# Merge and output projection as a planned list, their loads through the tile of x, the first two row blocks in two parts

## The chip, the core and the metric

The kernel runs on one core of a Trainium2 chip. The metric is the device time of one execution in microseconds (us). The core has five engines that work side by side: PE (TensorE, matmuls), DVE (VectorE), ACT (ScalarE), POOL (GpSimd) and SP (SyncE, which here issues nearly all DMA transfers). Each takes its instructions in a fixed order; semaphores tie them together.

## What is computed

One layer of a diffusion backbone over 512 tokens of width 1024: a token mixer (a long convolution of width 512 and an RWKV-7 recurrence of width 512, merged by gates, then an output projection) and an expert-choice mixture of 16 experts. What matters here is the end of the mixer and the start of the experts:

```python
y_hy = hyena_branch(hy_cols, p) @ p['hy_proj']                 # (512, 512) @ (512, 1024)
y_rw, finals = rwkv_branch(rw_cols, p, states0)
g_hy, g_rw = jnp.split(jax.nn.sigmoid(gate_cols), 2, axis=-1)
mixed = (g_hy * y_hy + g_rw * (y_rw @ p['rw_proj'])) @ p['w_out']   # (512, 1024) @ (1024, 1024)
x = x + m_lat[2] * rmsnorm(mixed, p['norm1_post'])
h2 = rmsnorm(x, p['norm2_pre']) * (1.0 + m_lat[4]) + m_lat[3]
x = x + m_lat[5] * rmsnorm(expert_choice_moe(h2, p), p['norm2_post'])
# expert_choice_moe: softmax(h2 @ router_w); each expert takes its 64 best tokens; SwiGLU of width 2048
```

## The kernel before

The kernel runs through sections one after the other. Norm, modulation and the Hyena branch come first; the branch leaves its result in DRAM as u_d. Then comes the RWKV section. Its instructions are not issued as they are written: while `plan.on` is set, an object `Plan` records them (`Plan.add`, with an estimated cost and latency for each), and `Plan.run` sorts them by a list scheduler (for each engine, the instruction that can start first, and among those the one with the longest chain behind it) and issues them in that order inside `tc.manual_schedule()`. Consecutive matmuls that nothing cuts apart are one operation of the list; `cut()` ends such an operation. Because the issue goes through that one place, all instructions of this section stand under line 313 in the profile. The section also computes the gate columns (`gates`, lines around 890): weights of w_in pass through two raw tiles of 512 KB, the tanh of the result goes by a staging tile `stg` to g_d in DRAM. The recurrence's result, after its epilogue, goes to y_d.

Behind it, from line 1296 on, stands what the change edits. These instructions are not planned by hand; the framework's own scheduler orders them, and it may issue them between those of the list.

- Merge (lines 1352 to 1382): q = 0 for the Hyena branch (u_d, hy_proj), q = 1 for RWKV (y_d, rw_proj). Each input of 128 x 512 and each weight block of 128 x 1024 is loaded into one of two raw tiles (pool `raw`, NRAW = 2) and split by `parts` into a high part (rounded to fp32r, on ACT) and a low part (the rest, on DVE). `mm3` multiplies high by high, high by low and low by high, 12 matmuls for each of 8 column blocks i. For q = 0 the gated result goes to `first` (the place of `xn`), for q = 1 the two are added on POOL and split again into `mixT`.
- The weights' parts stand in the five 2 MB places of pool `w2p`: hy_proj in 0 and 1, rw_proj in 2 and 3, the halves of w_out in 4, 0 and 1, 2. The expert weights use these five places after that, two of `w3p` and the one of x (`xp`), eight in all, in turn; the first in turn before is place 3.
- Output projection (lines 1385 to 1431): for each of four row blocks n of 128 tokens and each half q of 512 channels, 24 matmuls over 8 channel blocks k into one of four PSUM banks; then the norm (Square on ACT with its sum, Sqrt, reciprocal), scaling and adding to x on DVE, transposes, the router's matmuls `pl`, and the norm of the new x.
- Router and experts (from line 1440 on, unchanged): softmax, the 64 best tokens of each expert by eight rounds of MAX8 and MATCH_REPLACE8 on DVE, then for each of 8 pairs of experts a gather by one-hot matmuls (`px`), three weight loads of 2 MB for each quarter of an expert (lines 1513 and 1516) and the matmuls `ph` and `py`.

Pools of the framework are placed on the left or the right side of SBUF. A pool that takes over the place of a closed one waits for all of it, unless it is opened with `reuse_waits="tile"`, as the RWKV section's pool `rw` is; then each tile waits for the tiles that it overlaps alone.

## Time and profile before

| | |
|---|---|
| median of 3 runs | 1858.79 us (1856.28 to 1859.96) |
| profiled execution | 1859.19 us |
| its span, first to last instruction | 1857.4 us |
| mean granted TensorE clock | 0.944 |
| PE, DVE, ACT, POOL busy | 86%, 35%, 20%, 11% |
| RWKV section | about 350 to 741 us |
| merge and output projection | about 741 to 870 us |
| router and experts | about 870 to 1857 us |

Times in the rows are microseconds from the span's start unless marked ns. L328, L333, L334, L337, L340 and L370 are helper lines (matmul, ACT copy, ACT function, tensor by tensor, scalar-tensor-tensor, transpose); what an instruction is for is read from its tile names, out<-in. `ppr` is the merge's PSUM, `po` that of the output projection, `gg` the gate tile, `mixh` and `mixl` the parts of mixT, `yr` and `yh` an input and its high part, `exp_w` an expert's weights. PEclk is the granted clock as a share of 2.4 GHz. A bracket holds the idle time of the engine ahead of the instruction and what ended it.

### The profile page before, as it was taken

Reading aid. Unit: us, or ns where it says so; the run is one execution under the profiler, and the core shown is the slowest. Engines: PE = TensorE matmul, PEld = TensorE weight load, DVE = VectorE, ACT = ScalarE, POOL = GpSimd, SP = SyncE. Lnnn points to the kernel's source line nnn. Section 1 sums busy time; section 2 is a strip of 40 time slices with the busy share of each in tenths; the row PEclk is TensorE's granted clock in tenths of the full one; section 3 lists DMA queues with packets and bytes.
Section 4 is the critical chain, followed back from the end, with each engine's and each line's share of the span. In section 5 each row is a group of like instructions: output and inputs, shape, how many; then the busy total and the mean of one; then the engine's idle time right before and its main releaser. Section 6 shows DMA issues by size and latency. Waiting matters only on the chain.

```text
span 1857.4 us, 33304 instructions
## 1 busy us (share of the span) xinstructions
PE 1600.7 (86%) x14486; PEld 1054.1 (57%) x14486; DVE 643.1 (35%) x1230; ACT 373.2 (20%) x773; POOL 209.0 (11%) x222
## 2 busy tenths in 40 slices
PE   7898899777788999688699989989899898998985
PEld 3456676555666776477565545455454554555542
DVE  3765665566776533454402002011020110200203
ACT  4444432232343212233000000000000000000001
POOL 0534201312333201020000000000000000000001
PEclk8799899888898999799799999999999999999998
DMA  7455443465554532754699999999999999999995
GB/s 289 142 178 187 159 151 131 145 158 133 118 124 121 140 81 82 253 176 185 287 427 426 427 427 427 425 427 426 428 426 427 426 426 427 427 427 427 426 426 228
DMA packets 168382, 537.36 MB, mean 289 GB/s; under 512 B 96827, under 2 KB 110795, under 8 KB 143404
## 3 DMA queue, kind: packets, MB, share of 16 engines
q1 hardware_dynamic: 166064, 531.72, 74.5%
q10 hardware_dynamic: 2172, 3.51, 0.6%
q8 instruction: 114, 1.87, 0.4%
q14 instruction: 32, 0.26, 0.0%
HBM read 507.89 MB, written 27.30 MB: 288 GB/s over the span
## 4 chain that ended last, share of the span: by engine, by line
PE 40%; DMA 14%; DVE 3%; issue 1%; ACT 1%; POOL 0%; DVEq 0%; SPq 0%; ACTq 0%; POOLq 0%
PE ph L328 18%; DMA exp_w<-in_exp_w 12%; PE py L328 10%; PE px L328 3%; PE pso L328 3%; PE po L328 2%; PE pht L370 1%; DVE hd L337 1%; ACT hT L333 1%; PE ppr L328 1%; PE pl L328 0%; PE pbq L328 0%; PE pbp L328 0%; POOL gg L337 0%; DMA gg<-g_d 0%
## 5 line engine op out<-in xcount | busy, mean ns | idle before, releaser
L328 PE MATMUL ph<-exp_w,xe 128*64 128x256 f32 x4096 | 470.0, 381 | 25.3 <-DMA exp_w<-in_exp_w 25.3
L328 PEld LDWEIGHTS ph<-exp_w,xe 128*64 128x64 f32 x4096 | 319.0, 137 | 193.9 <-issue 66.5
L337 DVE TENSOR_TENSOR hd<-ph,hd 128x256 f32<-128x256 f32 x64 | 27.2, 425 | 672.8 <-PE ph L328 672.8
L328 PE MATMUL py<-exp_w,hT 128*64 128x512 f32 x1024 | 236.8, 598 | 24.6 <-ACT hT L333 24.6
L313 PE MATMUL psfl<-hh,raw 128*128 128x256 f32 x512 | 149.6, 423 | 14.9 <-DMA raw<-in_w_in 8.5
L328 PEld LDWEIGHTS py<-exp_w,hT 128*64 128x64 f32 x1024 | 78.3, 136 | 138.4 <-issue 92.8
L313 PEld LDWEIGHTS psfl<-hh,raw 128*128 128x128 f32 x512 | 95.9, 204 | 37.9 <-issue 16.1
L334 ACT ACTIVATE hd<-ph 128x256 f32<-128x256 f32 x64 | 24.6, 384 | 432.6 <-PE ph L328 432.6
L333 ACT ACTIVATE hT<-pht 128x256 f32<-128x256 f32 x64 | 24.6, 384 | 283.6 <-PE pht L370 283.6
L328 PEld LDWEIGHTS px<-OH,xn 128*128 128x128 f32 x512 | 66.2, 198 | 23.4 <-issue 22.4
L1495 POOL COPY sel<-kcon 16x128 f32<-16x128 f32 x8 | 2.2, 283 | 609.4 <-PE pbq L328 609.4
L328 PE MATMUL pso<-ye,oT 128*128 128x512 f32 x128 | 69.5, 634 | 0.7 <-ACT ye L333 0.7
L328 PE MATMUL px<-OH,xn 128*128 128x128 f32 x512 | 68.5, 283 | 0.9 <-DVE OH L344 0.9
L370 PE MATMUL pht<-kcon,hd 128*128 128x128 f32 x128 | 28.0, 300 | 36.1 <-DVE hd L337 35.9
L337 DVE TENSOR_TENSOR mo<-pso,mo 128x512 f32<-128x512 f32 x56 | 38.4, 691 | 40.9 <-PE pso L328 40.9
L370 PEld LDWEIGHTS pht<-kcon,hd 128*128 128x128 f32 x128 | 12.8, 140 | 65.1 <-DVE hd L337 65.1
L337 POOL TENSOR_TENSOR mw<-mw 128x256 f32<-128x256 f32 x32 | 35.0, 1110 | 97.0 <-DVE mw L340 90.8
L1539 DVE COPY ye<-py 64x512 f32<-64x512 f32 x16 | 11.1, 693 | 95.7 <-ACT ye L333 95.7
L313 DVE TENSOR_TENSOR M<-pssc,kcon 128x256 f32<-128x256 f32 x80 | 29.2, 416 | 24.8 <-PE pssc L313 23.5
L340 DVE SCALAR_TENSOR_TENSOR mw<-mw,sc,mw 128x256 f32<-128x256 f32 x64 | 28.5, 493 | 22.9 <-DMA mw<-in_mod_w 21.4
L328 PE MATMUL phy<-ha,wh_h 128*128 128x512 f32 x96 | 31.0, 455 | 1.9 <-ACT wh_h L333 1.8
L313 PE MATMUL pslv<-XX,M 32*32 32x32 f32 x1152 | 17.6, 209 | 16.0 <-issue 7.4
(383 smaller groups left out, 2227.3 us busy)
## 6 DMA issues: line engine op xcount, KB each, us to landing
exp_w<-in_exp_w SPq DMA_DIRECT2D x192, 2048.0 KB
mw<-in_mod_w SPq DMA_DIRECT2D x48, 512.0 KB
raw<-in_w_in SPq DMA_DIRECT2D x32, 512.0 KB
w_h<-in_w_in SPq DMA_DIRECT2D x12, 512.0 KB
w_c<-in_w_in SPq DMA_DIRECT2D x12, 512.0 KB
k<-k_d SPq DMA_DIRECT2D x8, 768.0 KB
g_d<-stg SPq DMA_DIRECT2D x16, 256.0 KB
gg<-g_d SPq DMA_DIRECT2D x16, 256.0 KB
```

The lines of the kernel that those rows point to most:

```text
L313: f(*a, **k)
L328: return TE.matmul(*a, **k)
L333: return A.activation(out, in_, func, scale=scale, **kw)
L334: return A.activation(out, in_, func, bias=bias, scale=scale, **kw)
L337: e.tensor_tensor(out, a, b, op=op)
L340: V.scalar_tensor_tensor(out, a, s, b, op0=op0, op1=op1)
L370: TE.transpose(out, in_, ident[0:n, 0:n])
L1495: G.tensor_copy(sel, ident[0:NE, 2 * q:2 * q + 2].rearrange("p (a b) -> p a b", b=1).to_broadcast([NE, 2, CAP]))
L1539: V.tensor_copy(ye[r, 512:1024], py[64:128, :])
```

## The change

Merge and output projection are recorded and issued by `Plan` as well, in a second list. Six places of 512 KB take their loads up to the twelfth (four of them in the tile of x, which is itself loaded later, and the two raw tiles), two after that; all loads go by SP. The first two row blocks are projected from channel blocks 0 to 5 first and from 6 and 7 later. The adds of the last three column blocks go to DVE. The ring of half-row tiles has five (NGT) and serves gates, scaled halves, transposed halves and the throw-away outputs of Square. Six pools now wait tile by tile, x's pool is on the right side, and four buffers of the RWKV section are created earlier. The planner's costs change too, for both lists: matmul operations, DMA cost (now the time that its bytes take) and latency (2.0 us), and no latency between two operations of PE. The diff, without the parts that only move a definition; from `first = xn` on the lines taken out (printed above) are left away:

```diff
-NGT = 3
+NGT = 5
...
-                place, t = None, 0.2 if what == "transpose" else size * (0.00055 if single else 0.00175) + 0.02
+                place, t = None, 0.2 if what == "transpose" else size * (0.00043 if single else 0.00175) + 0.015
             else:
                 place, t = (lhs.offset // lhs.ap[0][0], out.offset // out.ap[0][0]), 0.116 * size / 64
             if self.open is None:
-                self.open = dict(e=engine, calls=[], cost=0.15, small=[], lat=0.35, reads=[], writes=[])
+                self.open = dict(e=engine, calls=[], cost=0.05, small=[], lat=0.35, reads=[], writes=[])
                 self.ops.append(self.open)
...
-            cost, lat = 0.07, 2.2 + size / (180e3 if run >= 512 else 60e3)
+
+            cost, lat = max(0.07, size / (380e3 if run >= 512 else 100e3)), 2.0
...
-                o["cost"] += sum(t for _, t in o["small"]) / min(4, len(set(p for p, _ in o["small"])))
+                o["cost"] += 0.1 + sum(t for _, t in o["small"]) / min(4, len(set(p for p, _ in o["small"])))
...
-            o["rank"] = o["cost"] + max((o["lat"] + ops[j]["rank"] for j in o["succ"]), default=0.0)
+            o["rank"] = o["cost"] + max(((0.0 if ops[j]["e"] == o["e"] == "tensor" else o["lat"]) + ops[j]["rank"] for j in o["succ"]), default=0.0)
...
-                p["from"] = max(p["from"], s + o["cost"] + o["lat"])
+                p["from"] = max(p["from"], s + o["cost"] + (0.0 if p["e"] == o["e"] == "tensor" else o["lat"]))
...
+            for key, shape in (("hh", [P, KD, T // 2]), ("stg", [P, T]), ("gm2", [P, P]), ("v8", [P, 8])):
+                buf(key, shape)
...
-    w2p = ctx.enter_context(tc.tile_pool(name="w2p", bufs=NW2, side="right"))
+    w2p = ctx.enter_context(tc.tile_pool(name="w2p", bufs=NW2, side="right", reuse_waits="tile"))
...
-    xp = t2.enter_context(tc.tile_pool(name="xp", bufs=1))
+    xp = t2.enter_context(tc.tile_pool(name="xp", bufs=1, side="right", reuse_waits="tile"))
     xs = xp.tile([P, 4096], F32, tag="w2", name="xs").rearrange("p (n d) -> p n d", n=4)
-    mp = t2.enter_context(tc.tile_pool(name="moe", bufs=1))
+    mp = t2.enter_context(tc.tile_pool(name="moe", bufs=1, reuse_waits="tile"))
     xn = mp.tile([P, 4, D], F32, name="xn")
     sm = mp.tile([P, 4, 8], F32, name="sm")
     rt = mp.tile([P, KD, NE], F32, name="rt")
     x1_d = tc.dram_tile([4, P, D], F32, name="x1_d")
 
-    EW = [[(V, G)[i] for i in x] for x in EWS]
-
-    def halves(w, k, name, es):
+    def halves(w, k, name, hl):
 
         src = w.rearrange("(k p) f -> p k f", p=P)
         f = src.shape[2]
         n = max(1, 1024 // f)
-        hl = [wchunk(f"w{t_}_{name}").bitcast(F32R).rearrange("p (k f) -> p k f", k=k) for t_ in "hl"]
+        hl = [x.bitcast(F32R).rearrange("p (k f) -> p k f", k=k) for x in hl]
         for i in range(0, k, n):
-            raw = raw_tile(f"w_{name}{i}").rearrange("p (k f) -> p k f", k=n)
+            raw = raws2().rearrange("p (k f) -> p k f", k=n)
             SY.dma_start(out=raw, in_=src[:, i:i + n])
-            parts(hl[0][:, i:i + n], hl[1][:, i:i + n], raw, es[i // n % len(es)])
+            parts(hl[0][:, i:i + n], hl[1][:, i:i + n], raw)
         return hl
 
-    def mm3(pt, lhs, rhs, steps):
+    def mm3(pt, lhs, rhs, steps, first=True, last=True):
 
         for i, (a, b) in enumerate(steps):
-            mm(pt, lhs[0][a], rhs[0][b], start=i == 0, stop=False)
+            mm(pt, lhs[0][a], rhs[0][b], start=first and i == 0, stop=False)
             mm(pt, lhs[0][a], rhs[1][b], start=False, stop=False)
+            cut()
         for i, (a, b) in enumerate(steps):
-            mm(pt, lhs[1][a], rhs[0][b], start=False, stop=i == len(steps) - 1)
+            mm(pt, lhs[1][a], rhs[0][b], start=False, stop=last and i == len(steps) - 1)
+            if i % 2:
+                cut()
 
 
     with ExitStack() as e4:
-        op = e4.enter_context(tc.tile_pool(name="op", bufs=1))
+        op = e4.enter_context(tc.tile_pool(name="op", bufs=1, reuse_waits="tile"))
+        rings.clear()
         mixT = [op.tile([P, KD, T], F32R, name=f"mix{t_}") for t_ in "hl"]
         m2row = op.tile([P, D], F32, name="m2row")
+        yh = [[op.tile([P, 4, T], F32R, name=f"y{t_}{q}") for t_ in "hl"] for q in range(2)]
+        rtm = op.tile([P, 2, KD, NE], F32, name="rtm")
+        rts = op.tile([P, NE], F32, name="rts")
+        all1 = op.tile([P, P], F32, name="all1")
+        lg = mp.tile([P, 4, NE], F32, name="lg")
+        wk = [wchunk(f"wk{i}") for i in range(NW2)]
 
         first = xn.rearrange("p n d -> p (n d)").rearrange("p (k t) -> p k t", t=T)
+        pxx = lambda: turns("px", lambda name: bank(("h1", "h3")[int(name[-1]) % 2], 2, name), 4)
+        rows2 = [raw_tile(f"raw2_{i}") for i in range(NRAW)]
+        passes = [0]
+        def raws2():
+            passes[0] += 1
+            some = [xs[:, n, :] for n in range(4)] + rows2 if passes[0] < 13 else rows2
+            return some[passes[0] % len(some)]
+        half = lambda: turns("gt", lambda name: op.tile([P, T], F32, name=name), NGT)
+        tr = lambda: turns("tr", lambda name: bank("tr", 2, name), 2)
+        pl = bank("so", 1, "pl")
+        plan.on = True
+        for q, (dram, w) in enumerate(((u_d, "hy_proj"), (y_d, "rw_proj"))):
+            for g in range(0, 4, 2):
+                raw = raws2().rearrange("p (g t) -> p g t", g=2)
+                SY.dma_start(out=raw, in_=dram[g:g + 2].rearrange("g p t -> p g t"))
+                parts(yh[q][0][:, g:g + 2], yh[q][1][:, g:g + 2], raw)
+            ww = halves(I[w][0], 4, w, wk[2 * q:2 * q + 2])
+            if q:
+                SY.dma_start(out=m2row, in_=m_d[0:1, :].to_broadcast([P, D]))
+                n1row = raws2()
+                SY.dma_start(out=n1row, in_=I["norm1_post"][0:1, :].to_broadcast([P, D]))
+                stt(m2row, m2row, 0.5, n1row, ALU.mult, ALU.mult)
+            for i in range(KD):
+                gt = half()
+                SY.dma_start(out=gt, in_=g_d[2 * i + q])
+                pt = pxx()
+                mm3(pt, ww, yh[q], [((slice(None), k, slice(i * P, (i + 1) * P)), (slice(None), k)) for k in range(4)])
+                stt(gt if q else first[:, i, :], gt, 1.0, pt, ALU.add, ALU.mult)
                 if q:
+                    tt(V if i > 4 else G, gt, gt, first[:, i, :], ALU.add)
+                    parts(mixT[0][:, i, :], mixT[1][:, i, :], gt)
+        wo = [halves(I["w_out"][0][:, q * 512:(q + 1) * 512], KD, f"o{q}", [wk[(4 + 2 * q + i) % NW2] for i in range(2)]) for q in range(2)]
+        SY.dma_start(out=rt, in_=I["router_w"][0].rearrange("(k p) e -> p k e", p=P))
+        for n in range(4):
+            SY.dma_start(out=xs[:, n, :], in_=I["x"][0, n * P:(n + 1) * P, :])
         for v, a in enumerate((modA[:, 1, :, 0], mcol[:, 2, :, 0])):
             tt(V, rtm[:, v], rt, a.rearrange("p (k o) -> p k o", o=1).to_broadcast([P, KD, NE]), ALU.mult)
         V.tensor_reduce(out=rts, in_=rtm[:, 1].rearrange("p k e -> p e k"), axis=AX.X, op=ALU.add)
         G.memset(all1, 1.0)
+        pt = tr()
         mm(pt[:, 0:NE], all1, rts, start=True, stop=True)
         V.tensor_copy(rts, pt[:, 0:NE])
+        outs = {}
+        def project_out(n, ks, first, last):
+            for q in range(2):
+                if first:
+                    outs[n, q] = pxx()
+                mm3(outs[n, q], mixT, wo[q], [((slice(None), k, slice(n * P, (n + 1) * P)), (slice(None), k)) for k in ks], first, last)
+        for n in range(2):
+            project_out(n, range(0, KD - 2), True, False)
         for n in range(4):
             s_ = sm[:, n, :]
+            if n < 2:
+                project_out(n, range(KD - 2, KD), False, True)
+            else:
+                project_out(n, range(KD), True, True)
             for q in range(2):
+                act(half(), outs[n, q], AF.Square, scale=0.5, accum=s_[:, q:q + 1])
             tt(V, s_[:, 0:1], s_[:, 0:1], s_[:, 1:2], ALU.add)
             act(s_[:, 1:2], s_[:, 0:1], AF.Sqrt, bias=par[:, 54:55], scale=1.0 / D)
             V.reciprocal(s_[:, 1:2], s_[:, 1:2])
             for q in range(2):
                 f = slice(q * 512, (q + 1) * 512)
+                mx = half()
+                stt(mx, outs[n, q], s_[:, 1:2], m2row[:, f], ALU.mult, ALU.mult)
+                tt(V, xs[:, n, f], xs[:, n, f], mx, ALU.add)
+                pt = tr()
                 for k in range(4):
                     transpose(pt[:, k * P:(k + 1) * P], xs[:, n, q * 512 + k * P:q * 512 + (k + 1) * P])
+                xT = half().rearrange("p (k t) -> p k t", t=P)
+                V.tensor_copy(xT.rearrange("p k t -> p (k t)"), pt)
+                for k in range(4):
+                    mm(pl[:, n * NE:(n + 1) * NE], xT[:, k, :], rtm[:, 0, 4 * q + k, :], start=q + k == 0, stop=q + k == 4)
+                cut()
             SY.dma_start(out=x1_d[n], in_=xs[:, n, :])
+            for q in range(2):
+                act(half(), xs[:, n, q * 512:(q + 1) * 512], AF.Square, accum=s_[:, 2 + q:3 + q])
+            tt(V, s_[:, 2:3], s_[:, 2:3], s_[:, 3:4], ALU.add)
             act(s_[:, 2:3], s_[:, 2:3], AF.Sqrt, bias=par[:, 54:55], scale=1.0 / D)
             V.reciprocal(s_[:, 2:3], s_[:, 2:3])
             stt(lg[:, n, :], pl[:, n * NE:(n + 1) * NE], s_[:, 2:3], rts, ALU.mult, ALU.add)
             if n == 3:
                 act(s_[:, 7:8], s_[:, 2:3], AF.Exp, scale=0.0)
             act(xn[:, n, :], xs[:, n, :], AF.Copy, scale=s_[:, 2:3])
+        plan.run(tc)
+    mp = t2.enter_context(tc.tile_pool(name="moe2", bufs=1, reuse_waits="tile"))
     mo = mp.tile([P, 4, D], F32, name="mo")
     posm = mp.tile([NE, T], F32, name="posm")
     affT = mp.tile([NE, T], F32, name="affT")
+    w3p = t2.enter_context(tc.tile_pool(name="w3p", bufs=NW3, reuse_waits="tile"))
     slots[:] = [w2p] * NW2 + [w3p] * NW3 + [xp]
     chunks[0] = 0
     sx = mp.tile([P, 4, 3], F32, name="sx")
```

## Rows read from the trace of the kernel before

**Rows 1.** Stages: busy us (count) of PE, PEld, DVE, ACT, POOL, clock, DMA share
```profile
core 0: us, PE busy (x) PEld busy (x) DVE busy (x) ACT busy (x) POOL busy (x), PEclk, DMA share, GB/s
...
740.00:760.00 20.00, 1.18 (x3) 0.83 (x3) 4.46 (x6) 4.94 (x7) 0.00 (x0) 0.59 0.78 248
...
809.00:825.00 16.00, 11.06 (x38) 8.23 (x37) 8.63 (x14) 5.19 (x9) 5.67 (x4) 0.79 0.76 275
...
1100.00:1700.00 600.00, 541.25 (x3730) 307.85 (x3726) 74.08 (x168) 40.00 (x96) 1.13 (x4) 1.00 1.01 427
```

**Rows 2.** PE in order of time, 755 to 915: start, us, operation, count
```profile
758.82 0.79 PE L328 MATMUL ppr<-yh,wh_hy_proj 128*128 128x512 f32 x1 [18.93 <-DMA w_hy_proj<-in_hy_proj]
...
764.11 0.41 PE L328 MATMUL ppr<-yh,wh_hy_proj 128*128 128x512 f32 x1
...
864.45 0.39 PE L328 MATMUL po<-wh_o,mixh 128*128 128x512 f32 x1
...
868.18 2.03 PE L328 MATMUL po<-wh_o,mixl 128*128 128x512 f32 x8
...
909.79 1.08 PE L328 MATMUL ph<-exp_w,xe 128*64 128x256 f32 x6
```

**Rows 3.** What PE waited for, 740 to 915: us in total, times, longest
```profile
PE ppr L328 <- DMA w_hy_proj<-in_hy_proj: 18.9, 1, 18.9
...
PE po L328 <- ACT mixh L333: 4.9, 2, 3.5
...
PE ppr L328 <- ACT yh L333: 1.8, 2, 1.5
```

**Rows 4.** Issues on SP's queue in order of time: start, us, line, transfer
```profile
735.04 0.42 SPq L1358 DMA_DIRECT2D yr<-u_d  x1
...
741.55 0.45 SPq L313 DMA_DIRECT2D g_d<-stg  x1
...
754.12 0.93 SPq L1331 DMA_DIRECT2D w_hy_proj<-in_hy_proj  x2
...
864.64 0.33 SPq L1516 DMA_DIRECT2D exp_w<-in_exp_w  x1
...
874.76 1.19 SPq L1513 DMA_DIRECT2D exp_w<-in_exp_w  x2
...
915.11 0.33 SPq L1516 DMA_DIRECT2D exp_w<-in_exp_w  x1
```

**Rows 5.** ACT and DVE in order of time, at the seam and in row block 0
```profile
739.92 0.60 ACT L313 ACTIVATE stg<-psfl 128x512 f32<-128x512 f32 x1 [2.81 <-PE psfl L313]
...
745.25 0.63 ACT L333 ACTIVATE yh<-yr 128x512 fp32r<-128x512 f32 x1 [4.73 <-DMA g_d<-stg]
...
834.45 0.60 ACT L334 ACTIVATE mx<-po 128x512 f32<-128x512 f32 x1 [8.14 <-PE po L328]
...
836.98 1.41 DVE L340 SCALAR_TENSOR_TENSOR mx<-po,sm,m2row 128x512 f32<-128x512 f32 x2
```

**Rows 6.** Groups of instructions, 735 to 870: busy us, mean ns | idle before, releaser
```profile
L337 POOL TENSOR_TENSOR gg<-gg,xn 128x512 f32<-128x512 f32 x8 | 13.6, 1716 | 63.8 <-DMA w_o<-in_w_out 54.7 <-DVE gg L340 9.1
...
L333 ACT ACTIVATE wh_o<-w_o 128x1024 fp32r<-128x1024 f32 x8 | 8.3, 1050 | 3.1 <-DMA w_o<-in_w_out 3.1
...
L337 DVE TENSOR_TENSOR xs<-xs,mx 128x512 f32<-128x512 f32 x6 | 3.9, 684 | 0.0
```

**Rows 7.** Stages of the RWKV section, columns as in the first group
```profile
400.00:600.00 200.00, 156.47 (x3736) 122.86 (x3738) 137.38 (x289) 67.57 (x181) 58.02 (x67) 0.89 0.54 127
600.00:741.00 141.00, 135.44 (x2688) 104.36 (x2682) 60.58 (x135) 34.95 (x74) 22.68 (x29) 0.98 0.39 101
```

**Rows 8.** What SP's queue waited for, 361 to 740: us in total, times, longest
```profile
SPq L313 <- PE psfl L313: 105.0, 15, 14.2
```

**Rows 9.** What the gate matmuls of the RWKV section sat idle for
```profile
  DMA raw<-in_w_in: 8.5, 2
```

More of the change, by code (lines that the diff above doesn't have):

```diff
@@ L387, in program, with turns @@
     y_d = tc.dram_tile([4, P, T], F32, name="y_d")
+    rings = {}
+    def turns(key, make, n):
+        r = rings.setdefault(key, [[], 0])
+        if len(r[0]) < n:
+            r[0].append(make(f"{key}_{len(r[0])}"))
+        r[1] += 1
+        return r[0][(r[1] - 1) % n]
     cz_d = tc.dram_tile([12, P, S], F32, name="cz_d")
@@ L837, in program @@
             HR = (slice(0, 64), slice(64, 128))
-            rings = {}
-            def turns(key, make, n):
-                r = rings.setdefault(key, [[], 0])
-                if len(r[0]) < n:
-                    r[0].append(make(f"{key}_{len(r[0])}"))
-                r[1] += 1
-                return r[0][(r[1] - 1) % n]
             def buf(key, shape, n=1):
@@ L1344, in program @@
     with ExitStack() as e4:
-        op = e4.enter_context(tc.tile_pool(name="op", bufs=1))
+        op = e4.enter_context(tc.tile_pool(name="op", bufs=1, reuse_waits="tile"))
+        rings.clear()
         mixT = [op.tile([P, KD, T], F32R, name=f"mix{t_}") for t_ in "hl"]
         m2row = op.tile([P, D], F32, name="m2row")
-        first = xn.rearrange("p n d -> p (n d)").rearrange("p (k t) -> p k t", t=T)
-        with ExitStack() as e3:
-            pj = e3.enter_context(tc.tile_pool(name="pj", bufs=1))
-            for q, (dram, w) in enumerate(((u_d, "hy_proj"), (y_d, "rw_proj"))):
-                yh = [pj.tile([P, 4, T], F32R, name=f"y{t_}{q}") for t_ in "hl"]
-                def inputs():
-                    for g in range(4):
-                        yr = raw_tile(f"yr{q}{g}")[:, 0:T]
-                        SY.dma_start(out=yr, in_=dram[g])
-                        parts(yh[0][:, g, :], yh[1][:, g, :], yr)
-                if q == 0:
-                    inputs()
-                ww = halves(I[w][0], 4, w, EW[q])
-                if q:
-                    inputs()
-                    for n in range(4):
-                        SY.dma_start(out=xs[:, n, :], in_=I["x"][0, n * P:(n + 1) * P, :])
-                    A.dma_start(out=rt, in_=I["router_w"][0].rearrange("(k p) e -> p k e", p=P))
-                    A.dma_start(out=m2row, in_=m_d[0:1, :].to_broadcast([P, D]))
-                    n1row = raw_tile("n1row")
-                    A.dma_start(out=n1row, in_=I["norm1_post"][0:1, :].to_broadcast([P, D]))
-                    stt(m2row, m2row, 0.5, n1row, ALU.mult, ALU.mult)
-                    dump("m2row", m2row)
-                for i in range(KD):
-                    gt = pj.tile([P, T], F32, tag="gt", bufs=NGT, name=f"gg{i}{q}")
-                    SY.dma_start(out=gt, in_=g_d[2 * i + q])
-                    pt = pxx(f"ppr{i}{q}")
-                    mm3(pt, ww, yh, [((slice(None), k, slice(i * P, (i + 1) * P)), (slice(None), k)) for k in range(4)])
-                    stt(gt if q else first[:, i, :], gt, 1.0, pt, ALU.add, ALU.mult)
-                    if q:
-                        tt(G, gt, gt, first[:, i, :], ALU.add)
-                        parts(mixT[0][:, i, :], mixT[1][:, i, :], gt)
@@ L1385, in program @@
-        wo = [halves(I["w_out"][0][:, q * 512:(q + 1) * 512], KD, f"o{q}", EW[2]) for q in range(2)]
-        op = e4.enter_context(tc.tile_pool(name="op2", bufs=1))
-        rtm = op.tile([P, 2, KD, NE], F32, name="rtm")
+        yh = [[op.tile([P, 4, T], F32R, name=f"y{t_}{q}") for t_ in "hl"] for q in range(2)]
[3 more added lines that the diff above has]
+        lg = mp.tile([P, 4, NE], F32, name="lg")
@@ L1400, in program @@
+        for n in range(2):
+            project_out(n, range(0, KD - 2), True, False)
         for n in range(4):
             s_ = sm[:, n, :]
-            pts = []
-            mx = op.tile([P, D], F32, tag="mx", bufs=2, name=f"mx{n}")
+            if n < 2:
+                project_out(n, range(KD - 2, KD), False, True)
+            else:
+                project_out(n, range(KD), True, True)
             for q in range(2):
-                pt = pxx(f"po{n}{q}")
-                mm3(pt, mixT, wo[q], [((slice(None), k, slice(n * P, (n + 1) * P)), (slice(None), k)) for k in range(KD)])
-                act(mx[:, q * 512:(q + 1) * 512], pt, AF.Square, scale=0.5, accum=s_[:, q:q + 1])
-                pts.append(pt)
+                act(half(), outs[n, q], AF.Square, scale=0.5, accum=s_[:, q:q + 1])
```

21 lines of the change are left out of this document (removed).

## Prediction

> **What bounds the kernel now.** I read the stages first. From 1100 to 1700 us the expert stage keeps the DMA engines at a share of 1.01 and 427 GB/s, with PE busy 541 of 600 us [rows 1]. One expert load is 2 MB, so 4.9 us at that rate; the loop issues 16 x 4 x 3 = 192 of them, 943 us. The end is therefore the moment at which this stream gets going, plus a fixed length. SP's queue shows when that is: eight places are filled ahead of time, and the ninth load leaves only at 915.11, when PE has read the first place [rows 4], 5.3 us after the first expert matmul at 909.79 [rows 2]. So a microsecond off that matmul's start is a microsecond off the end, provided the eight places are full by then.
>
> From the end of the last output projection matmul (868.18 + 2.03 = 870.2) to the first expert matmul there are 39.6 us [rows 2]: row block 3's norm, the router, the top-64 search and the gather. The change leaves all but the first few of these as they are. What it edits lies before 870.2: merge and output projection, on PE from 758.8, 111.4 us. Ahead of it PE stands still for 18.9 us [rows 3], at a granted clock of 0.59 of the full 2.4 GHz in that stretch [rows 1].
>
> By the code, the merge has 2 x 8 x 12 = 192 matmuls and the output projection 4 x 2 x 24 = 192. Sixteen of them start between 864.45 and 868.18 [rows 2], one each 0.233 us, so 384 take 89.6 us of the 111.4; 4.9 + 1.8 = 6.7 us are waits [rows 3]; two stretches run at the half clock; transposes and router matmuls of row blocks 0 to 2 and small change are the rest, 10.1 us by difference. The first half-clock stretch is 758.82 to 764.11, 12 matmuls in 5.29 us instead of 2.80 [rows 2], 2.5 us lost. The second follows the 4.9 us of waits, in the stretch with clock 0.79 [rows 1]; I take the same 2.5 us for it.
>
> **The change part by part.** *Start of the merge, S.* Before, u_d and hy_proj go through the two raw tiles that the gates of the RWKV section hold to their end, and the first split also waited 4.73 us for a store of the pool that it takes over, g_d<-stg [rows 5]. After, six 512 KB places take all six loads of the first half (two of u_d, four of hy_proj), waits go tile by tile, and the four buffers used last are placed under tiles that are written later. The early bound is S = 741: the last PSUM bank is read at 739.92 + 0.60 [rows 5], and the new PSUM pool waits for that. The late bound has SP issue nothing before its last store, 741.55 + 0.45 = 742.0 [rows 4]; 1 MB of u_d at the 248 GB/s of this stretch [rows 1] is 4.2 us, and from the first hy_proj issue to the first matmul went 758.82 - 754.12 = 4.7 us [rows 2, 4]: S = 750.9. For the early end speaks that SP issued a load of the merge at 735.04, ahead of the RWKV list's store at 741.55 [rows 4]; against it, that both sections are now fixed lists and that two of the six places are still the gates' raw tiles. I take 747, just past the middle.
>
> *Stream.* The waits on mixh came from POOL, whose adds take 1.72 us each [rows 6]. The last three of eight move to DVE at 0.68 us [rows 6], and row blocks 0 and 1 first multiply the six channel blocks that are ready, 4 x 18 matmuls or 16.8 us of cover for the last two. So 4.9 us and the half clock behind them go; with rw_proj's loads no longer queued behind two tiles, so do the 1.8. At worst half of the 6.7 stays, and with it the 2.5.
>
> *New waits.* The second half of w_out can be split only once rw_proj's high part is free, as before; its last two pieces take two raw tiles twice, about 9 us, under those 16.8 us: nothing on the path. Four banks are now held by blocks 0 and 1, so block 2 must wait for block 0's: from its last Square to the end of the first scaling goes 834.45 to 836.98 + 0.70 = 3.2 us [rows 5], against 12 matmuls (2.8 us) left of block 1. That is 0.5 us if the list finishes block 0 first, 3.3 if both finish together; I take 1.5. Every later matmul is queued behind it.
>
> *What costs nothing.* Three loads move from ACT's queue to SP's, each below 1 us of issue, in a stretch where SP mostly waits; x is loaded after w_out instead of before, wanted only some 40 us later. Squares in halves add one short ACT and one DVE instruction for each row block, under the next block's matmuls; for block 3 the first half is done early, and scaling and adding by halves lets its transposes begin sooner: -0.5 us (0 to -1.5).
>
> *Expert loads.* Three of eight were issued by 864.64 [rows 4], since place 3 came first in turn; now place 0 does, and it is read until block 3. If all eight start where the next ones did, 874.76 [rows 4] or 4.6 us after the final matmul, 8 x 4.9 and some 2 us from issue to landing (4.7 above less a split of 1.05 [rows 6] and 512 KB at 248 to 427 GB/s leaves 1.5 to 2.4) put the last at 45.8, against 39.6 + 5.3 = 44.9 for the ninth issue: 1 us late, less if the first leave earlier. I put 0, at most 1.
>
> *New costs in the planner* also re-order the RWKV section. There PE is busy 156 of 200 us up to 600 and 135 of 141 after it [rows 7]. Gate matmuls drawn into the first stretch would shorten the second; a load believed shorter than it is makes PE stand. The trace shows neither order. I take 0, with ends -10 (a quarter of the 43.5 idle us filled) and +8.5, as much again as PE now waits for gate weights [rows 9].
>
> **Sum.** Stream 111.4 - 6.7 - 2.5 + 1.5 = 103.7; 747 + 103.7 = 850.7 against 870.2, that is 19.5 earlier, and with the tail 20. The profiled execution took 1859.19 us, 0.4 above the median of 1858.79; 1859.2 - 20 = 1839.
>
> Of TensorE's clock a page has a say. The row shows half-rate matmuls after the 18.9 us gap, and I leave those 2.5 us in, as S = 747 still leaves a gap of 7. The Trainium skill (TensorE: Matmul & The Clock Gate, "Why this matters for your kernels") lets the clock drop only after a sufficiently long idle gap; by that rule S = 741 would also give 2.5 us back, and 1839 would become 1830.5. The trace agrees for the two gaps it has here: behind both the matmuls run at half rate.
>
> **Rivals.** *A, loads run ahead.* The first half's loads all sit in place when the RWKV section ends: S = 741, no cold start, bank wait 0.5. 741 + 111.4 - 6.7 - 5.0 + 0.5 = 841.2, 29 earlier: 1830. The issue at 735.04 speaks for it.
>
> *B, fixed order turns into stalls.* S at its late end, half the waits and their clock loss left, the bank wait at 3.3: 750.9 + 111.4 - 3.4 + 3.3 = 862.2, 8 earlier: 1851. For it: a list stops at its first late operand, where the scheduler of before also fixed an order but by a different estimate.
>
> *C, slower.* The RWKV list is where the loss would arise. SP's queue already waits 105 us for places of gate weights [rows 8]. If a merge load that waits for its place stands in that queue ahead of gate weights, or the list counts on weights too early, each of the 32 gate loads makes PE wait. The Trainium skill (DMA: Bandwidth & Descriptors, "Anatomy of one DMA") puts the wait on the issuing sequencer, not on the DMA engines; rows 8 agree. At 0.8 us each, 32 loads cost 26 us: 1839 + 26 = 1865. It decides from 20 us on, 0.63 us a load; against it, 2 loads cost 8.5 us in all now.
>
> *D, the two cancel.* The merge gains as in B and the RWKV section loses those 8.5: 1859.
>
> **How the numbers follow.** Forecast (1832 to 1847) 0.44; A 0.22; B 0.17; C 0.06; D 0.06; 0.05 for a RWKV section shorter by its full 10 on top of A, 1820. Range: A less half of the RWKV gain, 1825, to B plus 2, 1853, which leaves out the last, C, D and some of A and B. A measurement tells 0.2% from no change, 3.7 us. Faster 0.44 + 0.22 + 0.17 + 0.05 = 0.88, within 0.06, slower 0.06.
>
> **What would show it.** Right: first merge matmul 741 to 751 after the old clock, no wait on mixh, last output projection matmul near 851, first expert matmul near 890, ninth expert load 5 us behind it, DMA at 427 GB/s after. Wrong: a RWKV end off 740 by more than 5 us; PE waits inside the merge of over 5 us; an expert stream that starts later than PE asks for it.

## The result, and the profile after

| | before | 350.0 | after |
|---|---|---|
| median, us (runs) | 1858.44 (4) | 1832.37 (4) |
| lowest to highest | 1856.28 to 1859.96 | 1825.73 to 1833.49 |
| ratio, 95% interval | | 0.9853 [0.9828, 0.9879] |
| profiled execution / its span | 1859.19 / 1857.4 | 1833.49 / 1831.7 |
| first merge matmul (S) | 758.82 | 738.07 |
| last output projection matmul ends | 870.21 | 843.33 |
| first expert matmul | 909.79 | 884.18 |

The change is worth 26.1 us by the medians and 25.6 us at the first expert matmul; I had forecast 20. The span shrank by 25.7, so behind that matmul nothing moved, as [rows 1, 4] had led me to expect. Stages of after; columns are the stretch, its us, and busy us (count) of PE, PEld, DVE, ACT, POOL, then the granted clock, DMA share and GB/s:

```profile
400.00:600.00 200.00, 163.16 (x4005) 128.51 (x4005) 148.06 (x304) 74.58 (x201) 65.67 (x78) 0.89 0.58 138
600.00:741.00 141.00, 123.14 (x2413) 98.53 (x2414) 59.20 (x125) 37.56 (x64) 14.96 (x18) 0.97 0.42 120
1100.00:1700.00 600.00, 541.44 (x3738) 310.79 (x3737) 76.97 (x175) 39.54 (x95) 1.13 (x4) 1.00 1.01 426
```

The expert stage is the one of [rows 1]. The RWKV section is not that of [rows 7]: PE does 6.7 us more work in the loose stretch up to 600. What PE waited for from 730 to 915 in after (us in total, times, longest), to be set beside [rows 3]:

```profile
PE px L314 <- ACT wk L314: 11.3, 1, 11.3
PE px L314 <- DVE xn L314: 3.1, 2, 2.0
PE tr L314 <- DVE xs L314: 3.0, 1, 3.0
...
PE px L314 <- DVE gt L314: 0.4, 1, 0.4
```

The 18.9 us ahead of the merge became 11.3. The 4.9 us on mixh are gone, and so is any wait of row block 2 for a PSUM bank. New are 3.1 us on DVE, which reads the merge's banks into xn: it reads the first of four at 763.91 and the other three from 766.25, each time behind the split of a weight of 1.23 us. PE in order of time (start, us, operation, count, and in brackets the idle time before it with what ended it):

```profile
738.07 0.80 PE L314 MATMUL px<-yh,wk 128*128 128x512 f32 x1 [11.27 <-ACT wk L314]
...
742.46 0.39 PE L314 MATMUL px<-yh,wk 128*128 128x512 f32 x1
...
764.73 0.47 PE L314 MATMUL px<-yh,wk 128*128 128x512 f32 x1 [2.02 <-DVE xn L314]
...
766.98 0.80 PE L314 MATMUL px<-yh,wk 128*128 128x512 f32 x1 [1.08 <-DVE xn L314]
...
773.12 0.40 PE L314 MATMUL px<-yh,wk 128*128 128x512 f32 x1
...
842.16 1.17 PE L314 MATMUL px<-wk,mixl 128*128 128x512 f32 x4
...
843.17 1.85 PE L314 MATMUL pl<-rtm,gt 128*128 128x16 f32 x16
...
884.18 1.08 PE L329 MATMUL ph<-exp_w,xe 128*64 128x256 f32 x6
```

Two half-rate stretches are left, to 742.46 and from 766.98 to 773.12; the second now stands behind the waits on xn. SP's queue shows why the gap ahead of the merge is still 11.3:

```profile
720.61 5.69 SPq L314 DMA_DIRECT2D raw<-in_hy_proj  x2
727.92 0.38 SPq L314 DMA_DIRECT2D g_d<-stg  x1
728.39 0.42 SPq L314 DMA_DIRECT2D y_d<-Y  x1
728.86 1.29 SPq L314 DMA_DIRECT2D xs<-u_d  x2
...
889.51 0.33 SPq L1532 DMA_DIRECT2D exp_w<-in_exp_w  x1
```

Two loads of hy_proj run ahead, the second only when the last gate frees its raw tile at 725.97 (the 5.69 us span both issues). u_d comes behind the last two stores. ACT then starts to split u_d and the later weights:

```profile
734.16 1.06 ACT L314 ACTIVATE yh<-xs 128x1024 fp32r<-128x1024 f32 x1 [3.67 <-DMA xs<-u_d]
735.67 1.06 ACT L314 ACTIVATE yh<-xs 128x1024 fp32r<-128x1024 f32 x1 [0.45 <-DMA xs<-u_d]
736.96 1.06 ACT L314 ACTIVATE wk<-xs 128x1024 fp32r<-128x1024 f32 x1 [0.23 <-DMA xs<-in_hy_proj]
```

The last of these ends the gap.

**Where the 25.6 us come from.** I split the path at three points. The RWKV section's work on PE ends at S less the idle time printed beside it: 758.82 - 18.93 = 739.9 before, 738.07 - 11.27 = 726.8 after. So the section's end gives 13.1, the gap 18.9 - 11.3 = 7.6, the stream (first merge matmul to the end of the last one of the output projection) 111.4 - 105.3 = 6.2 (from exact values), and the tail (from there to the first expert matmul) takes back 40.9 - 39.6 = 1.3. Of the 13.1, 1.0 is there already at the section's first matmul, 349.98 before and 349.02 after; the section itself gives 12.1. So nearly half of the gain sits in the term that I had put at 0. The section from its first matmul on PE to its last, in before, after and a second profile of after (e13); columns as above:

```profile
349.98:739.89 389.91, 329.29 (x6744) 255.39 (x6744) 227.09 (x475) 124.44 (x311) 94.83 (x112) 0.90 0.51 126
349.02:726.80 377.78, 318.77 (x6744) 251.85 (x6744) 228.31 (x475) 126.19 (x313) 96.03 (x113) 0.91 0.52 131
345.13:719.32 374.19, 317.34 (x6744) 251.61 (x6744) 228.49 (x475) 126.38 (x313) 96.19 (x113) 0.92 0.52 132
```

The same split for every kernel that was run, from its profiled execution, with its median:

| kernel | RWKV starts | RWKV ends | gap | stream | tail | median us |
|---|---|---|---|---|---|---|
| before | 350.0 | 739.9 | 18.9 | 111.4 | 39.6 | 1858.4 |
| after | 349.0 | 726.8 | 11.3 | 105.3 | 40.9 | 1832.4 |
| e1 costs alone | 348.8 | 723.0 | 17.4 | 111.1 | 39.7 | 1840.4 |
| e2 old costs for the RWKV list | 349.8 | 736.7 | 10.9 | 103.9 | 40.8 | 1842.0 |
| e5 load cost alone | 350.3 | 722.9 | 19.1 | 110.8 | 39.8 | 1843.5 |
| e6 PE costs alone | 347.5 | 763.5 | 18.5 | 112.9 | 39.7 | 1882.5 |
| e3 two places | 347.0 | 719.9 | 12.5 | 106.9 | 39.2 | 1838.0 |
| e10 buffers late | 347.8 | 723.0 | 12.1 | 103.6 | 40.3 | 1830.3 |
| e12 whole-pool waits | 348.5 | 722.4 | 11.8 | 105.7 | 41.0 | 1830.7 |
| e8 blocks whole | 350.1 | 727.2 | 11.5 | 105.2 | 39.7 | 1828.9 |
| e9 adds on POOL | 344.8 | 720.5 | 11.4 | 103.2 | 40.6 | 1833.4 |
| e11 neither | 349.4 | 724.1 | 11.4 | 106.3 | 39.3 | 1826.4 |
| e13 after again | 345.1 | 719.3 | 11.8 | 104.2 | 40.7 | 1828.5 |
| e7 loads before the end | 350.9 | 727.8 | 4.1 | 102.5 | 39.4 | 1823.9 |

Beside them the kernel before took 1858.2, 1858.5 and 1861.0 us (medians). The profiled executions of e3 and e9 are the fastest of their runs, 10.1 and 8.5 us below the median beside them. The ends need care: the order of the RWKV section's instructions is the same in after, e1, e3 and e7 to e13 (in e7 but for the queue of two stores), and yet its end lies anywhere from 719.3 to 727.8, mean 723.4. Much of this is there before the section begins: its first matmul comes between 344.8 and 350.9, and no edit of any run touches the work ahead of it. From that matmul to the end the ten profiles take 373.0 to 377.8 us, mean 375.3. Before and e2 share the old order: 389.9 and 387.0 us. So a difference of 5 us between two single ends says nothing on this section, and the section's length, the gap and the stream are read by themselves.

### The profile page after: what moved, and what is told of

It reads as the page before. It is cut to its first block, busy times and chain, and to the rows that moved or that the text cites. A ratio compares the mean times of both kernels' runs of the same rounds, so it can differ in the third digit from the quotient of the medians.

```text
span 1831.7 us, 33298 instructions
## 1 busy us (share of the span) xinstructions
PE 1584.9 (87%) x14486; PEld 1048.7 (57%) x14486; DVE 647.7 (35%) x1233; ACT 376.6 (21%) x779; POOL 204.3 (11%) x219
## 4 chain that ended last, share of the span: by engine, by line
PE 60%; DMA 19%; DVE 10%; issue 4%; POOL 2%; ACT 2%; SPq 1%; DVEq 0%; ACTq 0%; POOLq 0%
PE ph L329 18%; DMA exp_w<-in_exp_w 12%; PE py L329 10%; PE psfl L314 4%; PE px L329 3%; PE pcl L329 3%; PE pso L329 3%; PE px L314 3%; PE pssc L314 2%; DMA mw<-in_mod_w 2%; PE psst L314 2%; PE pht L371 1%; DVE hd L338 1%; DVE gs L314 1%; SPq L314 1%
## 5 line engine op out<-in xcount | busy, mean ns | idle before, releaser
L314 PE MATMUL psfl<-hh,raw 128*128 128x256 f32 x512 | 142.5, 418 | 19.3 <-DMA raw<-in_w_in 12.5
L314 PE MATMUL px<-yh,wk 128*128 128x512 f32 x128 | 44.0, 421 | 14.4 <-ACT wk L314 11.3
L338 DVE TENSOR_TENSOR mo<-pso,mo 128x512 f32<-128x512 f32 x56 | 38.4, 691 | 39.3 <-PE pso L329 39.3
L314 PEld LDWEIGHTS px<-yh,wk 128*128 128x128 f32 x128 | 26.0, 203 | 22.5 <-ACT wk L314 12.1
```

The source lines that it names most:

```text
L314: f(*a, **k)
L338: e.tensor_tensor(out, a, b, op=op)
```

## The experiments

**e1, e2, e5, e6: do the planner's costs make the RWKV gain, and which?** e1 is before with all new costs. e5 and e6 are before with one part each:

```diff
-            cost, lat = 0.07, 2.2 + size / (180e3 if run >= 512 else 60e3)
+            cost, lat = max(0.07, size / (380e3 if run >= 512 else 100e3)), 2.0   # e1, e5
-                self.open = dict(e=engine, calls=[], cost=0.15, ...
+                self.open = dict(e=engine, calls=[], cost=0.05, ...               # e1, e6
...
```

(e6 has the other PE lines of the change too: 0.43 ns a column, 0.1 us for a group of small matmuls, no latency between two operations of PE.) e2 is after with the old costs for the RWKV list and the new ones for the second list.

> The kernel before, with the planner's new costs (matrix operations, loads, no latency between two operations of PE) and nothing else of the change, so that only the order of the RWKV list can differ. Theory 1 (the new costs shorten the RWKV section by 13 us, and it is worth the same at the end): last output store on SP near 728 instead of 740.7, first expert matmul near 897, time 1858.4 - 13 = 1845, give or take 3. Rival 2 (the 13 us come from elsewhere in the change, from the buffers placed early or from the merge's loads in the queue): section ends within 3 us of 740, time within 3 us of 1858.

Measured: 1840.37, ratio 0.9913 [0.9895, 0.9931]. The time is 1.6 us below theory 1's stretch, and rival 2 is out. The section takes 374.3 us and ends at 723.0, and it is nearly all that moved: gap and stream are within 1.6 us of before's, and the waits on mixh are 5.1 us.

> The kernel after, with the old costs for the RWKV list and the new ones for the list of merge and output projection. Theory 1 (costs make the 13 us of the RWKV section): section ends near 741 as before, the rest of the gain, 25.6 - 13.1 = 12.5 us, stays: 1845 to 1846. Rival 2: section still ends near 728, time within 3 us of 1832. Rival 3 (the two gains are not additive, since a later end of the RWKV section lets the merge's loads come in under it): between 1836 and 1842.

Measured: 1841.97, ratio 0.9915 [0.9890, 0.9940]. The section takes 387.0 us and ends at 736.7, while gap and stream keep their gain (8.0 and 7.5 us here). So the costs shorten the RWKV section by some 13 us (388.4, the mean of the two lengths in the old order, less 375.3), and the list of merge and output projection gives the rest without them. The time itself lies in rival 3's stretch and below theory 1's, but not for rival 3's reason: the gap is 10.9 us, hardly less than after's 11.3. By the times the costs alone give 17.9 us (e1) and the rest alone 16.2 (e2), 34 together, against 26.1 and 32.5 for the whole in two sessions; the spread of the section is in each of these figures.

> The kernel before with only the new cost and latency of a load in the planner. All the new costs alone gave 18 us. Theory L (the loads' cost makes it: with the size charged to the queue instead of to the landing, the planner starts the gate weights and the recurrence's transfers at other times): 10 us or more, time at or below 1848. Rival M (the cost of PE's operations makes it): within 4 us of before, 1854 to 1862. Both in part: 1849 to 1853.

Measured: 1843.46, ratio 0.9924 [0.9899, 0.9950]; the section takes 372.6 us and ends at 722.9. Theory L holds: the load's cost alone gives all of it.

> The kernel before with only the new costs of PE's operations in the planner (0.05 us instead of 0.15 for each operation, a column at 0.43 ns instead of 0.55, no latency between two operations of PE). Theory M: 10 us or more, time at or below 1848. Rival L: within 4 us of before, or above it, since gates believed cheaper are drawn in where the recurrence needs PE. Both in part: 1849 to 1853.

Measured: 1882.50, ratio 1.0137 [1.0108, 1.0166], 24 us slower: neither theory had this size, though rival L left room above. The section takes 416.0 us and ends at 763.5. What PE waited for in it, in e6 (361 to 765), the two largest:

```profile
PE pslv L313 <- DMA XX<-X_d: 17.6, 14, 4.1
PE psfl L313 <- DMA raw<-in_w_in: 12.1, 1, 12.1
```

and the same two in before and in e5:

```profile
PE psfl L313 <- DMA raw<-in_w_in: 8.5, 2, 6.3
...
PE pslv L313 <- DMA XX<-X_d: 6.3, 7, 2.2
```

```profile
PE psfl L313 <- DMA raw<-in_w_in: 9.3, 2, 6.2
```

In e5 the waits on XX, 64 KB transfers of the recurrence, are 0.9 us in all. With PE's operations cheaper and the loads at their old price, the order that comes out makes PE stand for these transfers 14 times instead of 7. The two waits are 14.9 us longer than in before, of the 26 by which the section is longer; the wait for gate weights is no mark of e6, since after has 12.5 us of it. The granted clock over the section is 0.85 in e6, against 0.90 in before and 0.93 in e5. It is the pair of costs that has to fit; in the change the load's part more than makes up for what PE's part alone would lose.

**e3, e10, e12: what cut the gap from 18.9 to 11.3?** Three parts of the change bear on it; each is taken out alone.

```diff
-            some = [xs[:, n, :] for n in range(4)] + rows2 if passes[0] < 13 else rows2
+            some = rows2                                                # e3
...
-            for key, shape in (("hh", [P, KD, T // 2]), ("stg", [P, T]), ...
-                buf(key, shape)                                         # e10
...
-    xp = ...tile_pool(name="xp", bufs=1, side="right", reuse_waits="tile"))
+    xp = ...tile_pool(name="xp", bufs=1, side="right"))                 # e12, and five more pools
```

> The kernel after, with all loads of merge and output projection through the two raw tiles alone, none through the place of x. Theory P (the place of x is what cut the gap ahead of the merge from 18.9 to 11.3 us): first merge matmul back by 7 us or more, to 745 or later, time 1840 or more. Rival Q (the gap was cut by the loads' place in SP's order and by the waits by tile, and in after the loads through the place of x stand behind the last stores anyway): first merge matmul within 3 us of 738, time 1830 to 1836. In both, waits for splits may come back inside the stream, up to 3 us.

Measured: 1838.03, ratio 0.9886 [0.9853, 0.9918]; gap 12.5, stream 106.9. The place of x is worth 1.2 us of gap and at most 1.6 of stream (two profiles of after differ by 1.1 in the stream). (S itself came at 732.4, since this execution's RWKV section ended at 719.9; my expectation should have named the gap.) The median is 5.7 above after's, of which I can place only these 2.8 us; the profiled execution took 1827.93, the other three 1835.94 to 1840.26.

> The kernel after without the four buffers (hh, stg, gm2, v8) set up ahead of the RWKV list: the instruction order of every engine is the same, only places in SBUF and with them the waits differ. Theory B (these buffers, used to the very end, then lie under tiles that the merge writes first, so that splits and loads wait for the last stores again, as the first split of before did for 4.73 us): gap ahead of the first merge matmul 13 to 16 us instead of 11.3. Rival C (u's loads stand behind the last stores on SP in any case, so the place of the buffers is worth nothing): gap 10.5 to 12.5 us, time within what moves with the RWKV section's end, 1825 to 1840.

Measured: 1830.34, ratio 0.9842 [0.9796, 0.9888]; gap 12.1. At most 0.8 us.

> The kernel after with the six pools behind the RWKV section waiting for all that lay in their place, not tile by tile; orders are the same. The first load of u then waits on SP for the landing of the last store of y, and the first split on ACT for the stores too. Theory W (waits by tile are a main part of the shorter gap): gap 14 us or more instead of 11.3. Rival C (the order on SP alone sets the gap, a store lands in about 2 us and part of it was waited for anyway): 11 to 13.5 us. In neither does the expert stage change.

Measured: 1830.67, ratio 0.9853 [0.9818, 0.9888]; gap 11.8. u_d leaves 4.4 us behind the section's end instead of 2.1, but its first split starts 8.1 behind it instead of 7.4, since the transfer then takes less long: 3.7 us from issue to split against 5.3. At most 0.5 us.

So none of the three explains the 7.6 us. Nor does the order of loads and last stores: in e1, which has no second list and keeps 17.4 us, two loads of u_d precede the last stores as well. What differs is how many loads have to follow each other through the raw tiles. Before, each of the four inputs of 128 x 512 takes a whole raw tile, of which it fills half; in the change two inputs go into one place. SP's queue, and the splits of u_d's second half on ACT, in e1 (section's end at 723.04):

```profile
716.85 5.68 SPq L1358 DMA_DIRECT2D yr<-u_d  x2
724.16 0.37 SPq L313 DMA_DIRECT2D g_d<-stg  x1
...
728.71 1.19 SPq L1358 DMA_DIRECT2D yr<-u_d  x2
...
735.59 1.01 SPq L1331 DMA_DIRECT2D w_hy_proj<-in_hy_proj  x2
```

```profile
734.21 1.31 ACT L333 ACTIVATE yh<-yr 128x512 fp32r<-128x512 f32 x2 [5.74 <-DMA yr<-u_d]
```

and in e3, which has the same two raw tiles and no other place (section's end at 719.93):

```profile
713.74 5.74 SPq L314 DMA_DIRECT2D raw<-u_d  x2
721.06 0.36 SPq L314 DMA_DIRECT2D g_d<-stg  x1
...
725.45 0.85 SPq L314 DMA_DIRECT2D raw<-in_hy_proj  x2
```

In e1 the second half of u_d waits for the raw tiles behind the section's end, and hy_proj for the second half: it leaves 12.6 us behind the end. In e3 all of u_d is under way before the end, and hy_proj leaves 5.5 us behind it. Of these 7.0 us the first merge matmul keeps 4.8 (12.5 us behind the end against 17.4), since that load then takes longer to its split, 5.9 us against 3.7. So the trace gives the larger part of the shorter gap to the two inputs in one place. A run with that edit alone was not made.

**e7: the gap is SP's order.** If u_d stands late only because of the two stores and the second raw tile, the stores can go out on ACT's queue, and the places can be dealt so that the first six loads precede any that reuses a place:

```diff
-                SY.dma_start(out=g_d[i:i + 2, :, half * 256:...
+                (A if half and i > 12 else SY).dma_start(out=g_d[i:i + 2, :, half * 256:...
...
-                SY.dma_start(out=y_d[g], in_=y)
+                (A if g > 2 else SY).dma_start(out=y_d[g], in_=y)
...
-            some = [xs[:, n, :] for n in range(4)] + rows2 if passes[0] < 13 else rows2
+            seq = [xs[:, 0, :], xs[:, 1, :], rows2[1], xs[:, 2, :], xs[:, 3, :], rows2[0], ...]
+            some = rows2 if passes[0] > len(seq) else [seq[passes[0] - 1]]
```

> The kernel after, with the last store of g and the last store of y issued by ACT instead of SP, and the places dealt out so that the first six loads (two of u, four of hy_proj) stand on SP's queue ahead of any load that reuses a place. Theory S (the 11.3 us gap is SP's order: u and the later weights stand behind the last two stores and behind the second raw tile, which PE frees at 726): the six loads leave between 719 and 726.5, the first merge matmul comes near 732 instead of 738.07, time 5 to 7 us below after, 1826. Rival T (the splits on ACT, six of 1.06 us behind the last gate, end the gap): first matmul 735 to 737, time 1 to 3 us below. Rival U (the loads collide with the last gates' weights or ACT's two issues delay the splits): no gain, 1832 or more.

Measured: 1823.85 (1821.67 to 1827.15), ratio 0.9821 [0.9802, 0.9841]. SP's queue, then ACT, then PE in e7:

```profile
720.17 0.43 SPq L314 DMA_DIRECT2D xs<-u_d  x1
721.62 0.33 SPq L314 DMA_DIRECT2D raw<-in_hy_proj  x1
722.00 0.43 SPq L314 DMA_DIRECT2D xs<-u_d  x1
722.47 1.02 SPq L314 DMA_DIRECT2D xs<-in_hy_proj  x2
726.98 0.33 SPq L314 DMA_DIRECT2D raw<-in_hy_proj  x1
```

```profile
728.94 0.39 ACTq L314 DMA_DIRECT2D g_d<-stg  x1
729.42 0.42 ACTq L314 DMA_DIRECT2D y_d<-Y  x1
729.90 1.06 ACT L314 ACTIVATE yh<-xs 128x1024 fp32r<-128x1024 f32 x1 [0.99 <-ACT stg L314]
```

```profile
731.95 0.80 PE L314 MATMUL px<-yh,wk 128*128 128x512 f32 x1 [4.14 <-ACT wk L314]
...
737.66 0.40 PE L314 MATMUL px<-yl,wk 128*128 128x512 f32 x1
```

Theory S holds: the gap is 4.1 us, and what remains of it is ACT (the last gate, two issues, the first two splits). The RWKV section of this execution ended last of the ten, 1.0 us behind after's, and still the span is 10.4 us shorter: 7.1 from the gap, 2.7 from the stream (the wait on xn falls to 1.8 us, and no half-rate stretch follows it), 1.5 from the tail, less that 1.0. The tail's part is mostly the clock in the gather (below), not the edit. By the medians e7 is 8.5 and 4.7 us below the two sessions of after; the intervals of the ratios overlap, so the trace carries this verdict more than the times do. The stores' queue and the dealing of the places were not run apart.

**e8, e9, e11: what removed the waits on mixh?**

```diff
-        for n in range(2):
-            project_out(n, range(0, KD - 2), True, False)     # e8, e11: all four blocks whole
...
-                    tt(V if i > 4 else G, gt, gt, first[:, i, :], ALU.add)
+                    tt(G, gt, gt, first[:, i, :], ALU.add)    # e9, e11
```

> The kernel after with row blocks 0 and 1 multiplied whole, not first by six channel blocks. Read by the stretch from the first merge matmul to the last of the output projection, 105.3 us in after, since the end of the RWKV section moves by several us from one execution to the next under one and the same order. Theory H (the 16.8 us of cover are needed): a wait on mixh of 2 to 4 us comes back, with a half-clock stretch of 2.5 behind it, 109 to 112 us, time 4 to 6 us above after. Rival I (moving three adds to DVE is enough, the split does nothing): no wait on mixh over 1 us, 104 to 107 us, time within 3 us of 1832.

Measured: 1828.87, ratio 0.9844 [0.9813, 0.9875]; stream 105.2, wait on mixh 0.9 us.

> The kernel after with all eight adds of the merge on POOL, the split of row blocks 0 and 1 kept. Theory H (the 16.8 us of cover hide two more adds of 1.72 us on POOL): no wait on mixh, 104 to 107 us from first merge matmul to last of the output projection, time within 3 us of 1832. Rival J (the last adds on POOL end later than the cover, as in before): a wait on mixh of 3 to 5 us, 108 to 113 us, time 4 to 7 us above after.

Measured: 1833.44, ratio 0.9876 [0.9844, 0.9908]; stream 103.2, no wait on mixh.

> The kernel after with row blocks 0 and 1 whole and all eight adds on POOL, that is without either of the two edits meant for the last channels. Each alone made no difference to the stretch from the first merge matmul to the last of the output projection (105.2 and 103.2 us against 105.3). Theory H2 (either edit suffices, but one is needed): the wait on mixh comes back with 3 to 5 us and a half-clock stretch behind it, 109 to 113 us, time 1836 to 1840. Rival K (the list order with the splits behind each add is enough): wait on mixh under 1.5 us, 103 to 106.5 us, time 1826 to 1836.

Measured: 1826.35, ratio 0.9822 [0.9771, 0.9873]; stream 106.3. PE's waits in e11:

```profile
PE px L314 <- DVE gt L314: 1.5, 1, 1.5
PE px L314 <- ACT mixh L314: 0.5, 1, 0.5
```

All eight adds are on POOL and no block is split, and the 4.9 us of [rows 3] don't come back. Rival K holds. In e11 PE starts the output projection at 789.20 on the channels that are ready and runs 28 matmuls of it while POOL does the last four adds from 789.14 on; the list cuts every product at each channel and so deals this work out by itself. The two edits in the change that look made for it add the 1.1 us between 106.3 and after's 105.3, which is no more than the two profiles of after differ by (105.3 and 104.2). That the list does it is shown against e1 (5.1 us on mixh) only together with the cuts inside `mm3` and the ring of five half-row tiles, which were not taken out by themselves.

**e13: the kernel after once more.**

> The kernel after once more, for its spread. Theory V (the end of the RWKV section moves from one execution to the next under one and the same order, which is why the profiled ends were 719.9 to 726.8 for one order): last PE work of the section between 718 and 728, gap 11 to 12 us and first merge matmul to last output projection 103 to 106 us in any case, time 1826 to 1837. Rival (the difference between the ends belongs to the kernels' places in SBUF): the end within 1.5 us of 726.8 again.

Measured: 1828.52 (1825.16 to 1829.90), ratio 0.9839 [0.9803, 0.9876]. The RWKV section ended at 719.3, gap 11.8, stream 104.2. Theory V holds in its numbers: the ends of two executions of one kernel are 7.5 us apart. But 3.9 us of this stand ahead of the section (its first matmul at 345.13 instead of 349.02), and 3.6 are its own.

## Why the prediction was right, and where not

- **The bound and 1:1.** Right. First expert matmul -25.6, ninth expert load 5.3 us behind it as before (889.51), 426 GB/s afterwards, span -25.7.
- **RWKV section, taken at 0 with ends -10 and +8.5.** The step that failed. Its sign and size come from the planner's costs: some -13, outside the lower end, and the end of the section moved from 739.9 to 726.8, more than the 5 us that I had named as a sign of being wrong. I had bounded the gain by a quarter of PE's idle time from 400 to 600, and idle time was the wrong place to look: over the section PE is idle 59.0 us instead of 60.6, but busy 318.8 instead of 329.3, with the same 6744 matmuls. The gate matmuls alone take 142.5 us instead of 149.6 (512 in each). The wait for gate weights, which I had feared, did grow, from 8.5 to 12.5 us. That order could also change how much PE time the same matmuls take, I had not counted. The granted clock is part of it: 0.90 over the section in before, 0.91 in after, 0.92 in e13, 0.93 in e5. How large a part, and what makes the rest, is not settled.
- **Rival C, the RWKV list makes PE wait, 1865.** It was a fear at the right place: e6 loses more than that, at 1882. I had named gate weights as the operand; what grew most in e6 is PE's wait for the recurrence's XX. The complete change doesn't show it: with the new load cost beside PE's, the same wait is 2.0 us in after. I gave the rival 0.06 without having looked at the two halves of the costs separately.
- **S = 747.** In the old clock, with the RWKV section where it was, the gap of 11.3 gives 739.9 + 11.3 = 751.2, my late end (750.9). I took the middle because one load was seen to precede a store. Two of six do in after; the four that count stand behind the stores. That two inputs now share one place, I had counted only as six loads for six places; by e1 and e3 it is the larger part of the shorter gap. e7 shows that the early side was there to be had: 739.9 + 4.1 = 744.
- **Stream, 111.4 to 103.7; measured 105.3.** Right in size, half wrong in reason. The waits on mixh and yh went, 6.7 us, but neither the adds on DVE nor the split of row blocks is needed for it (e11). The wait of row block 2 for its banks, 1.5 us, did not come. In its place PE waits 3.1 us on xn, since the list runs four channel blocks abreast and then needs all four banks read at once, while DVE has splits of weights ahead of the reads; the half-clock stretch that I had taken off came back behind it.
- **Tail, -0.5; measured +1.3.** Wrong in sign. Up to the gather OH x xn it is 0.9 us longer than before (0.6 in e3, e7 and e11): the list puts router matmuls of row block 2 behind the last projection matmul, 1.85 us at 843.17, where they stood ahead of it. The gather itself took 10.2 us in after, 9.8 in before and 8.9 in e3, at a granted clock of 0.71 in after and 0.82 in e3; that part moves from one execution to the next.
- **Expert loads at 0.** Right: the ninth still leaves when PE has read the first place.
- **The sum.** 13.1 + 7.6 + 6.2 - 1.3 = 25.6 against my 0 + 11.9 + 7.7 + 0.5 = 20. That 1832 lies at the lower end of the forecast is luck in part: the 13.1 us that I had at 0 stand against 7.6 that the other three terms fell short. The time fell near rival A's 1830, and not for its reason: no six loads in place, and two half-rate stretches instead of none.

## What to carry to other kernels

When a change touches a planner's costs, the sections that it re-orders belong in the sum even if no line of theirs is edited; run each half of the costs by itself, since here one half alone lost 24 us and the other alone gave 15. Read a section by its length, and not by its end alone, since what runs ahead of it moves too. A load that fills only half of its place can cost one more round through the places. What stands late on an in-order queue is found by reading the queue backwards from the first operand that is missed: two stores moved to another queue and a few places dealt anew were worth 7 us of gap. An edit made for a wait should be taken out again once the work is listed: here the list had removed the wait already.

## What I had not expected of the hardware

One order of one section, run again and again, began between 344.8 and 350.9 us, took 373.0 to 377.8 us and ended between 719.3 and 727.8 us, and the kernel took 1825.16 to 1833.49 us in eight runs. What makes the difference was not traced.

The clock fell after shorter idle times than those I had seen. Behind 4.14 us (e7) the matmuls run at the lower level, 1.2 GHz, until 737.66, and behind 2.02 us, some 1 us of work and 1.08 us more (after) they do until 773.12. A single wait of 2.10 us in the repeat of after was enough too; the half rate begins 1.2 us behind its end:

```profile
759.93 0.50 PE L314 MATMUL px<-yh,wk 128*128 128x512 f32 x1 [2.10 <-DVE xn L314]
760.26 0.40 PE L314 MATMUL px<-yl,wk 128*128 128x512 f32 x1
...
761.12 0.80 PE L314 MATMUL px<-yh,wk 128*128 128x512 f32 x1
...
764.62 0.39 PE L314 MATMUL px<-yh,wk 128*128 128x512 f32 x1
```

Single waits of 1.83 (e2) and 1.85 us (e3) had the same behind them. One of 1.51 us (before, at 786.28) had not, nor had 1.27 and 0.48 us (e7); of the kernels with the second list only e7 has no such stretch inside its stream. Its gap of 4.1 us ahead of the merge still pays the slow start of [rows 2]. The Trainium skill (TensorE: Matmul & The Clock Gate, "Why this matters for your kernels") asks for a sufficiently long idle gap before the clock falls. The gaps here that were enough are shorter than the one that it names, and the measurement decides. A gap short enough to keep the clock ahead of the merge was not reached in any run.
